# A hybrid decoder trunk on one core: the decode step's state update moved to ScalarE and an adding transfer, and Strassen pairs widened from 14 to 16 K tiles

## The chip, the cores and the metric

The kernel runs on 1 core of one Trainium2 chip. The metric is the device time of one execution in microseconds (us), lower is better. A core has a matmul engine (TensorE, PE in the profile; PEld is its weight load), VectorE (DVE), ScalarE (ACT), GpSimd (POOL) and SyncE (SP). Engines run on their own and wait for each other by semaphores; each takes its instructions in a fixed order. POOL and SP also issue DMA transfers, which 16 DMA engines carry out.

## What is computed

Two layers of a decoder trunk, for a prompt of 512 tokens and 8 samples of one new token each, all in float32:

```python
h = rmsnorm(x, norm_g)
z = h @ w_in                                # 2048 x 8192
b_c, c_c, x_c, g_c, q, k, v, g_r = split_projection(z)
conv_y, new_buf = short_conv(c_c * x_c, conv_buf, conv_w)
y_conv = b_c * conv_y * jax.nn.silu(g_c)
...
o, new_S = retention(q, k, v, ret_S, retention_log_gamma())
...
x = x + jnp.concatenate([y_conv, y_ret], axis=-1) @ w_out
x = x + jax.nn.sigmoid(x @ w_pg) * (p_i @ w_ple)
```

The part called the decode step here is the retention of the 8 samples. Each has one new position, so with L = 1 a head's state and output are

```python
S_new = jnp.exp(log_gamma) * S + jnp.einsum('blhd,blhe->bhde', k, v)    # gamma S + k v
o = S_new applied to q                                                  # one vector per head
```

with 4 heads of 256 and gamma = 1 - 2^(-5-h) for head h. There are 2 layers x 4 heads x 8 samples = 64 such steps, each on a 256 x 256 state.

## The kernel before

**Tiling.** Activations are kept turned, 128 features x 520 columns a tile (512 prompt tokens and 8 samples); 2048 features are KT = 16 such K tiles. A column block of a weight is 128 wide, and `pair` (line 396) makes the outputs of two neighbouring column blocks together. Each operand is split into a high part of float32r and a low remainder, and one product of a weight tile with half of the columns (260) is three matmuls (`mm3`, lines 247 to 249): high by high, high by low, low by high. ScalarE writes the high half of a weight chunk and VectorE the low half (`split_w`, lines 229 and 230), into a ring `split` of SPLIT = 60 tiles; raw weights are loaded by SP into a ring `raw`.

**Plain and Strassen pairs.** A pair is 2 output blocks x 2 halves of the columns. `plain` makes all four products of every K tile. `strassen` (line 290) takes the first s K tiles as two halves of s/2 and makes 7 products of s/2 tiles with sums of weights (`add`, line 319, on VectorE) and sums of operands (`operand_sums`, prepared once a layer and kept in slots) in place of 8; the remaining 16 - s tiles go by four plain products each. With s = 16 there is no remainder: it takes three PSUM banks (a, b, d) in place of four, and the result that `c` held waits in a slot. Which s a pair has is in the lists `HEADS`, `CONVS`, `OUT_ROWS` and `GATES`, one per stage, with a list for each layer. The packing of the weights on the host follows the same lists.

**Stages of a layer.** Four heads (`retain`, line 817), each with pairs for q, k, v and the gate; eight convolution blocks with two pairs each (the loop over `j`); then the output projection and the gate projection. The prompt's retention runs in nine steps (`steps`) hung between later pairs.

**The decode step.** `retain` puts a head's 8 samples on the list `todo`; `sample` (line 789) is called at the end of each head's pair, in the middle of every second one, and in the middle of the convolutions' pairs. A call finishes the sample loaded by the call before and loads the next one. `sample_load` (line 768) brings the state `sret` and the rows of k and q, spread over 128 partitions (`kq`), into two slots by POOL's queue (`SIDE`). `sample_step` (line 774) then scales the state by gamma on ScalarE (line 776), adds k times v on VectorE (line 780, two halves of 256, with v per partition as a scalar), stores the state to `o_rets` and reduces state times q on VectorE (line 784, two reductions into `osum`). After the last convolution block `sample_norm` normalises `osum`.

**Order.** The order on each engine is made when the program is built, by a scheduler with priorities; instructions passed through `keep` stay in program order among themselves. POOL's queue carries the decode step's transfers, the retention's operands (`hs`), the spilled activations (`x1s`, `x2s`, `yc`, `ys`) and some small work. `slots` is a pool of NSLOT = 75 tiles of 128 x 520.

## Time and profile before

| | |
|---|---|
| device time, median of 3 runs | 2167.58 us (2167.56 to 2169.25) |
| span of the profiled execution, first to last instruction | 2167.3 us |
| granted TensorE clock, mean | 0.999 |
| DMA traffic | 387.31 MB, mean 179 GB/s |
| heads of layer 0 and 1 | about 50 to 450 us and 1100 to 1500 us |
| convolutions of layer 0 and 1 | about 450 to 710 us and 1500 to 1750 us |

The profile is of one execution. Its page gives the span, which the prediction uses as that execution's own time; the median of the runs lies 0.3 us above it. Rows of groups read: line, engine, operation, what it writes from what it reads, shapes and count, then the busy time in us and the mean duration of one in ns, then the time that the engine stood idle just before these instructions and what ended most of it. Rows of waits read: who waited, for whom, us in total, times, the longest in us. Rows by stretch give, for each engine, busy us and instructions in brackets. Matmuls overlap in the pipeline, so PE's busy time says little on its own; the number of matmuls in a stretch does.

### The profile page before, as it was taken

The numbers are of one execution on the slowest core, as the hardware profiler recorded it, in microseconds if no ns is written. First come the engines' busy times: TensorE is split into PE (matmuls) and PEld (weight loads), VectorE is DVE, ScalarE is ACT, GpSimd is POOL, SyncE is SP. The second block draws the span as 40 slices with busy tenths as digits, with TensorE's granted clock in tenths as the row PEclk, the third lists the DMA queues.
The fourth block names the chain that finished last, engine by engine and source line by source line (L and its number), as shares of the span: only waits on it lengthen the run. The fifth ranks groups of instructions, "written<-read, shape, count | busy, mean of one in ns | idle before, by whom it ended". The sixth has DMA issues, their size and how long they took to land. (4 is left out here: it accounts for less than half of the span.)

```text
span 2167.3 us, 48178 instructions
## 1 busy us (share of the span) xinstructions
PE 2147.8 (99%) x17861; PEld 2142.1 (99%) x17861; DVE 1896.1 (87%) x3849; ACT 1264.5 (58%) x2647; POOL 430.6 (20%) x746
## 2 busy tenths in 40 slices
PE   9999999999999999999999999999999999999998
PEld 9999999999999999999999999999999999999998
DVE  8889988998999987987997988989999998879884
ACT  8656655565555655655765655565645555456565
POOL 2313222211001211200212222231111022011011
PEclk9999999999999999999999999999999999999999
DMA  8555565545543745645645566664464355566455
GB/s 288 171 175 197 181 217 184 178 157 175 158 129 118 238 156 187 215 154 160 215 144 175 172 213 191 189 209 170 151 182 149 120 158 202 176 207 200 128 164 198
DMA packets 182861, 387.31 MB, mean 179 GB/s; under 512 B 25888, under 2 KB 56352, under 8 KB 182624
## 3 DMA queue, kind: packets, MB, share of 16 engines
q1 hardware_dynamic: 128704, 212.98, 31.6%
q0 software_dynamic: 53056, 169.84, 23.8%
q8 instruction: 140, 2.29, 0.4%
q10 hardware_dynamic: 864, 1.39, 0.2%
q14 instruction: 97, 0.79, 0.1%
HBM read 318.96 MB, written 65.15 MB: 177 GB/s over the span
## 5 line engine op out<-in xcount | busy, mean ns | idle before, releaser
L247 PE MATMUL ps_g<-slot,split 128*128 128x260 f32 x5465 | 1531.6, 284 | 7.2 <-ACT slot L307 2.9
L248 PE MATMUL ps_g<-slot,split 128*128 128x260 f32 x5465 | 1534.3, 282 | 0.3 <-DVE slot L555 0.3
L249 PE MATMUL ps_g<-slot,split 128*128 128x260 f32 x5461 | 1519.9, 283 | 0.5 <-DVE split L230 0.5
L229 ACT ACTIVATE split<-raw 128x512 fp32r<-128x512 f32 (+2 forms) x1347 | 777.3, 596 | 583.1 <-DVE raw L319 213.2
L247 PEld LDWEIGHTS ps_g<-slot,split 128*128 128x128 f32 x5465 | 1024.0, 188 | 10.1 <-ACT slot L307 3.7
L248 PEld LDWEIGHTS ps_g<-slot,split 128*128 128x128 f32 x5465 | 1028.5, 188 | 0.5 <-DVE slot L555 0.5
L249 PEld LDWEIGHTS ps_g<-slot,split 128*128 128x128 f32 x5461 | 1019.8, 188 | 1.0 <-DVE split L230 1.0
L230 DVE TENSOR_TENSOR split<-raw,split 128x512 fp32r<-128x512 f32 (+2 forms) x1346 | 849.2, 652 | 172.5 <-PE ps_g L248 85.4
L319 DVE TENSOR_TENSOR raw<-raw 128x512 f32<-128x512 f32 (+1 forms) x660 | 428.9, 660 | 32.5 <-DMA raw<-wi 23.7
L307 ACT ACTIVATE slot<-ps_g 128x260 f32<-128x260 f32 x336 | 127.4, 381 | 140.6 <-PE ps_g L249 122.7
L551 ACT ACTIVATE slot<-slot 128x520 fp32r<-128x520 f32 (+1 forms) x212 | 109.2, 562 | 46.6 <-DVE slot L414 11.1
L552 DVE TENSOR_TENSOR slot<-slot,slot 128x520 fp32r<-128x520 f32 (+1 forms) x212 | 124.4, 620 | 4.1 <-ACT slot L551 3.9
L781 POOL DMA_DIRECT2D o_rets<-slot x64 | 35.3, 552 | 351.6 <-DVE slot L780 131.7
L307 DVE TENSOR_TENSOR slot<-ps_g,slot 128x260 f32<-128x260 f32 x168 | 70.9, 424 | 6.0 <-PE ps_g L249 3.7
L869 POOL DMA_DIRECT2D slot<-hs x64 | 46.2, 724 | 118.7 <-DVE split L230 42.7
L814 POOL DMA_DIRECT2D hs<-slot x64 | 35.6, 556 | 139.3 <-DVE slot L755 61.3
L780 DVE SCALAR_TENSOR_TENSOR slot<-slot,vs,slot 128x256 f32<-128x256 f32 x128 | 56.1, 481 | 4.5 <-ACT slot L776 4.3
L746 DVE TENSOR_TENSOR slot<-slot,slot 128x520 f32<-128x520 f32 x80 | 55.8, 698 | 4.7 <-DMA o_rets<-slot 3.7
L770 POOL DMA_DIRECT2D slot<-sret x64 | 35.5, 554 | 114.6 <-ACT split L229 37.3
L1058 POOL DMA_DIRECT2D slot<-x1s x76 | 40.8, 538 | 87.6 <-PE ps_g L249 27.2
L1209 POOL DMA_DIRECT2D x2s<-slot x30 | 16.4, 545 | 201.6 <-DVE slot L1204 200.6
L771 POOL DMA_DIRECT2D slot<-kq x64 | 34.9, 547 | 106.0 <-DVE slot L876 22.2
(217 smaller groups left out, 1733.8 us busy)
## 6 DMA issues: line engine op xcount, KB each, us to landing
raw<-wi SPq DMA_DIRECT2D x377, 256.0 KB, 3.9
raw<-wo SPq DMA_DIRECT2D x128, 256.0 KB, 5.4
raw<-wg SPq DMA_DIRECT2D x122, 256.0 KB, 4.1
raw<-wi SPq DMA_DIRECT2D x136, 192.0 KB, 4.0
slot<-x1s POOLq DMA_DIRECT2D x76, 260.0 KB, 5.1
slot<-sret POOLq DMA_DIRECT2D x64, 256.0 KB, 4.0
hs<-slot POOLq DMA_DIRECT2D x64, 256.0 KB, 4.0
slot<-hs POOLq DMA_DIRECT2D x64, 256.0 KB, 5.2
```

Source lines behind the costliest of these rows:

```text
L229: S.activation(hi, raw, AF.Copy)
L230: V.tensor_tensor(lo, raw, F(hi), SUB)
L247: PE.matmul(out, wh, xh, start=start, stop=False, skip_group_check=more)
L248: PE.matmul(out, wh, xl, start=False, stop=False, skip_group_check=more)
L249: PE.matmul(out, wl, xh, start=False, stop=stop, skip_group_check=more)
L307: fn(*args)
L319: V.tensor_tensor(out[:, n], x[:, n], y[:, n], op)
L551: keep(S.activation(hi, src[:, n], AF.Copy))
L552: V.tensor_tensor(lo, src[:, n], F(hi), SUB)
L746: V.tensor_tensor(out[:, n], v, table[:, n], MUL)
L780: keep(V.scalar_tensor_tensor(st[:, c], k, vs[:, h, e, b : b + 1], st[:, c], MUL, ADD))
L869: SIDE.dma_start(t[:, :512].rearrange("p (m n) -> p m n", m=2), src)
```

## The change

The decode step's sum gamma S + k v is formed in another way. ScalarE writes k times v into a fresh slot (two `Copy` activations of 256 with v as the scale), and a transfer of POOL's queue adds the state `sret` from DRAM onto it (`accum_op=ADD`). v is divided by gamma beforehand, so the slot then holds S_new / gamma; the reduction on VectorE multiplies by gamma, and ScalarE scales the slot by gamma before it is stored. A sample passes through three calls of `sample` in place of two: load k and q; add; reduce, scale and store. VectorE's two adds per sample are gone. The lists for heads and convolutions have 16 in place of 14, save the last pair of the convolutions; plain pairs and the pair with 8 stay. There is one slot more, the split ring has 56 tiles in place of 60, and the column vector `vec` is 128 wide in place of 160, since gamma is now a constant.

```diff
--- before.py
+++ after.py
@@ -27,7 +27,7 @@
 PLE = 256
 PAST = 4096
 EPS = 1e-6
-NSLOT = 75
+NSLOT = 76
 CH = 4
 CHS = 4
 CHA = 4
@@ -50,8 +50,9 @@
 EARLY = 6


-HEADS = [[0, 0, 0, 8] + [14] * 12, [0] + [14] * 15]
-CONVS = [[14] * 2 + [16] * 13 + [14]] * 2
+GAMMA = [1.0 - 2.0 ** (-5 - h) for h in range(H)]
+HEADS = [[0, 0, 0, 8] + [16] * 12, [0] + [16] * 15]
+CONVS = [[16] * 15 + [14]] * 2
 OUT_ROWS = [[0, 8, 16, 16, 16, 16, 16, 0]] * 2

 MIXED, MIX = 64, [*range(8, 14), *range(8), 14, 15]
@@ -62,7 +63,7 @@
 RAW = 32
 WARM = 8
 FIRST = 8
-SPLIT = 60
+SPLIT = 56


 def F(ap):
@@ -558,7 +559,7 @@
         return op


-    vec = const.tile([P, 160], F32, name="vec")
+    vec = const.tile([P, P], F32, name="vec")

     def norm_g(l, k):
         return vec[:, 16 * l + k : 16 * l + k + 1]
@@ -576,9 +577,6 @@
     def kd(h, m):
         c = 112 + 4 * h + m
         return vec[:, c : c + 1]
-
-    def gam(h):
-        return vec[:, 128 + h : 129 + h]

     ident = const.tile([P, P], F32, name="ident")
     ones = const.tile([P, P], F32, name="ones")
@@ -677,7 +675,7 @@
         if b == 1:
             raw = raw_ring.get(4)
             DMA.dma_start(raw.rearrange("p (m n) -> p m n", n=P), wi[0, 0:4, :, :P].rearrange("m p n -> p m n"))
-            S.dma_start(vec, vecs)
+            S.dma_start(vec, vecs[:, :P])
             x = get()
             for n in (LEFT, RIGHT):
                 DMA.dma_start(x[:, n], xT[0, :, n])
@@ -766,30 +764,36 @@
             return g

         def sample_load(h, b):
-            st, kb = get(), get()
-            SIDE.dma_start(st[:, :512], sret[l, h, b])
+            kb = get()
             SIDE.dma_start(kb[:, :512], kq[l, h, b].rearrange("c d -> (c d)").partition_broadcast(P))
-            return h, b, st, kb
-
-        def sample_step(h, b, st, kb):
-
-            keep(S.activation(st[:, :512], st[:, :512], AF.Identity, scale=gam(h)))
-            k = kb[:, 256:512]
+            return h, b, kb
+
+        def sample_add(h, b, kb):
+
+            st = get()
             for e in range(2):
                 c = slice(256 * e, 256 * e + 256)
-                keep(V.scalar_tensor_tensor(st[:, c], k, vs[:, h, e, b : b + 1], st[:, c], MUL, ADD))
-            SIDE.dma_start(o_rets[l, h, b], st[:, :512])
+                keep(S.activation(st[:, c], kb[:, 256:512], AF.Copy, scale=vs[:, h, e, b : b + 1]))
+            SIDE.dma_start(st[:, :512], sret[l, h, b], accum_op=ADD)
+            return h, b, kb, st
+
+        def sample_step(h, b, kb, st):
+
             for e in range(2):
                 c = slice(256 * e, 256 * e + 256)
-                V.tensor_tensor_reduce(k, st[:, c], kb[:, :256], 1.0, 0.0, MUL, ADD, osum[:, e, h, b : b + 1])
+                V.tensor_tensor_reduce(kb[:, 256:512], st[:, c], kb[:, :256], GAMMA[h], 0.0, MUL, ADD, osum[:, e, h, b : b + 1])
+            keep(S.activation(st[:, :512], st[:, :512], AF.Copy, scale=GAMMA[h]))
+            SIDE.dma_start(o_rets[l, h, b], st[:, :512])
             put(st, kb)

-        loaded = []
+        loaded, added = [], []

         def sample():

+            if added:
+                sample_step(*added.pop(0))
             if loaded:
-                sample_step(*loaded.pop(0))
+                added.append(sample_add(*loaded.pop(0)))
             if todo:
                 loaded.append(sample_load(*todo.pop(0)))

@@ -846,7 +850,7 @@
             vf = []
             for e, z in enumerate(head(mt + 4)):
                 t = z.slot if z.ps is None else copied(z.ps).slot
-                V.scalar_tensor_tensor(vs[:, h, e, :], t[:, SEQ:T], 1.0 / 16, rb[:, SEQ:T], MUL, MUL)
+                V.scalar_tensor_tensor(vs[:, h, e, :], t[:, SEQ:T], 1.0 / 16 / GAMMA[h], rb[:, SEQ:T], MUL, MUL)
                 vf.append(t)
             aside_copy(h, 4, vf)
             todo.extend((h, b) for b in range(NS))
@@ -1099,7 +1103,7 @@
             if j < CJ - 1:
                 middle.append(sample)
             if j == CJ - 1:
-                while loaded or todo:
+                while added or loaded or todo:
                     sample()
                 O.ready = 7
                 sample_norm(nc, small, pr, osum, onesd, half_neg, gs, lambda k: gn_g(l, k))
```

The scheduler orders the whole program anew. Of PE, 17664 rows become 17571.

The first place is SP's queue in the heads of layer 0, with the weight loads of the pairs. Line 312 (313 in the changed kernel) loads the halves of a Strassen pair's weights, line 222 (223) the K tiles left over. Before, from the pair with s = 8 through the first pair with s = 14:

```order
L312 DMA raw<-wi 128x512 x4
L222 DMA raw<-wi 128x512 x4
L312 DMA raw<-wi 128x384 x2
L312 DMA raw<-wi 128x512 x2
L312 DMA raw<-wi 128x384
L312 DMA raw<-wi 128x512
L312 DMA raw<-wi 128x384
L312 DMA raw<-wi 128x512
L222 DMA raw<-wi 128x256 x2
```

Now, from the pair with s = 8 to the last pair of the convolutions:

```order
L313 DMA raw<-wi 128x512 x4
L223 DMA raw<-wi 128x512 x4
L313 DMA raw<-wi 128x512 x216
L313 DMA raw<-wi 128x384 x2
L313 DMA raw<-wi 128x512 x2
```

The halves are 8 tiles in two loads of 4, and the loads of tiles left over are gone between the pair with 8 and the last pair.

The second place is one decode step in the convolutions of layer 0, the 28th of 64, on ScalarE and VectorE. ScalarE before, where line 776 scales the state by gamma:

```order
L229 ACTIVATE split<-raw 128x512
L776 ACTIVATE slot_417_7423<-slot_417_7423,vec 128x512
L307 ACTIVATE slot_421_7495<-ps_g 128x260
L229 ACTIVATE split<-raw 128x512 x3
L307 ACTIVATE slot_420_7494<-ps_g 128x260
```

ScalarE now, where line 785 scales the sample before this one and line 776 writes k times v of this one:

```order
L230 ACTIVATE split<-raw 128x512
L785 ACTIVATE slot_416_7261<-slot_416_7261 128x512
L776 ACTIVATE slot_421_7501<-slot_417_7265,vs 128x256 x2
L230 ACTIVATE split<-raw 128x512
L308 ACTIVATE slot_420_7335<-ps_g 128x260
L230 ACTIVATE split<-raw 128x512 x2
L308 ACTIVATE slot_419_7334<-ps_g 128x260
```

VectorE before, with the adds of line 780 and the reductions of line 784 (each of those also has a row that reads its sum out):

```order
L319 TENSOR_TENSOR raw<-raw 128x512 x2
L307 TENSOR_TENSOR slot_421_7495<-ps_g,slot_421_7495 128x260
L780 SCALAR_TENSOR_TENSOR slot_417_7423<-slot_418_7424,vs,slot_417_7423 128x256 x2
L319 TENSOR_TENSOR raw<-raw 128x512
L230 TENSOR_TENSOR split<-raw,split 128x512
L307 TENSOR_TENSOR slot_420_7494<-ps_g,slot_420_7494 128x260
L784 ISA slot_418_7424,osum<-slot_417_7423,slot_418_7424 128x256
L784 ISA osum 128x1
```

VectorE now, the same sample's reductions (slot_421_7501 is the slot that the transfer adds to):

```order
L231 TENSOR_TENSOR split<-raw,split 128x512 x3
L320 TENSOR_TENSOR raw<-raw 128x512
L231 TENSOR_TENSOR split<-raw,split 128x512 x4
L784 ISA slot_417_7265,osum<-slot_421_7501,slot_417_7265 128x256
L784 ISA osum 128x1
L784 ISA slot_417_7265,osum<-slot_421_7501,slot_417_7265 128x256
L784 ISA osum 128x1
L231 TENSOR_TENSOR split<-raw,split 128x512
L320 TENSOR_TENSOR raw<-raw 128x512 x2
```

The adds are gone. The reductions of this sample stand three weight splits behind the split that precedes its two copies on ScalarE, while the scaling by line 785 of the same sample comes a whole pair later.

The third place is POOL's queue around the same step. Before:

```order
L770 DMA slot_428_7909<-sret 128x512
L771 DMA slot_429_7910<-kq 128x512
L1112 DMA yc<-slot_414_7244 128x520
L781 DMA o_rets<-slot_417_7423 128x512
L771 DMA slot_434_8150<-kq 128x512
L770 DMA slot_433_8149<-sret 128x512
```

Now, where line 777 is the adding transfer and line 786 the store:

```order
L777 DMA slot_416_7261<-sret 128x512
L768 DMA slot_428_7751<-kq 128x512
L1116 DMA yc<-slot_413_7084 128x520
L786 DMA o_rets<-slot_416_7261 128x512
L777 DMA slot_421_7501<-sret 128x512
L768 DMA slot_433_7991<-kq 128x512
```

Before, a state's load stood samples ahead of its store and waited only for a slot; now its adding transfer stands right behind the store of the sample before, and both follow ScalarE's instructions of the same call.

## Prediction

> **What bounds the kernel now.** I read the first parts of the page, then busy time by stage, then the waits of PE.
>
> ```profile
> span 2167.3 us, 48178 instructions
> ## 1 busy us (share of the span) xinstructions
> PE 2147.8 (99%) x17861; PEld 2142.1 (99%) x17861; DVE 1896.1 (87%) x3849; ACT 1264.5 (58%) x2647; POOL 430.6 (20%) x746
> ```
>
> ```profile
> core 0: us, PE busy (x) PEld busy (x) DVE busy (x) ACT busy (x) POOL busy (x), PEclk, DMA share, GB/s
> 100.00:440.00 340.00, 340.00 (x2842) 339.93 (x2841) 306.35 (x677) 202.88 (x446) 89.32 (x154) 1.00 0.60 192
> 500.00:700.00 200.00, 200.00 (x1672) 200.00 (x1671) 181.12 (x359) 106.14 (x213) 23.30 (x32) 1.00 0.48 144
> 1180.00:1500.00 320.00, 319.33 (x2670) 318.83 (x2669) 285.91 (x640) 187.07 (x415) 84.51 (x143) 1.00 0.60 190
> ```
>
> ```profile
> PE ps_g L247 <- ACT slot L307: 2.9, 4, 1.3
> PE ps_g L247 <- ACT ps_g L307: 1.6, 2, 1.2
> PE ps_g L247 <- ACT split L229: 1.5, 2, 1.3
> ```
>
> The three stretches are the heads of layer 0, its convolutions, and the heads of layer 1. A matmul's busy time overlaps its neighbour's, so 99% alone proves little; the count does. The first stretch starts one matmul every 340.00 / 2842 = 119.6 ns and the second one every 200.00 / 1672 = 119.6 ns, at a granted clock of 1.00: the same pitch in two stages whose other work differs. PE's largest wait is 2.9 us in the whole run. So TensorE sets the end nearly everywhere, and time goes only with matmuls or comes back as new PE waits. VectorE is second, at 306.35 / 340.00 = 90.1% in the heads and 181.12 / 200.00 = 90.6% in the convolutions.
>
> **The matmuls.** A pair by `strassen` with s = 14 makes 7 products of 7 tiles and 4 products of the 2 tiles left over, (49 + 8) x 3 = 171 matmuls; with s = 16 it makes 7 x 8 x 3 = 168. The lists change 12 + 15 pairs of the heads and 2 + 2 of the convolutions: 31 pairs, 93 matmuls, 93 x 119.6 ns = **11.1 us** off PE. No cover is needed for this: PE is the bound, and in the convolutions 13 of 16 pairs already run at s = 16 with that same pitch.
>
> **VectorE, ScalarE and the queues.**
>
> ```profile
> L230 DVE TENSOR_TENSOR split<-raw,split 128x512 fp32r<-128x512 f32 x1031 | 695.0, 690 | 147.8 <-PE ps_g L248 81.2 <-ACT split L229 51.8 <-issue 6.1
> L319 DVE TENSOR_TENSOR raw<-raw 128x512 f32<-128x512 f32 x520 | 354.1, 688 | 17.6 <-DMA raw<-wi 12.1 <-DMA raw<-wo 2.9
> L230 DVE TENSOR_TENSOR split<-raw,split 128x384 fp32r<-128x384 f32 x249 | 137.1, 555 | 16.2 <-ACT split L229 9.9 <-PE ps_g L248 3.4 <-ACT slot L551 1.9
> L319 DVE TENSOR_TENSOR raw<-raw 128x384 f32<-128x384 f32 x140 | 77.4, 554 | 14.9 <-DMA raw<-wi 11.6 <-DMA raw<-wg 2.8
> L230 DVE TENSOR_TENSOR split<-raw,split 128x256 fp32r<-128x256 f32 x66 | 27.3, 423 | 8.5 <-ACT split L229 7.6 <-PE ps_g L248 0.8
> L307 ACT ACTIVATE slot<-ps_g 128x260 f32<-128x260 f32 x336 | 127.4, 381 | 140.6 <-PE ps_g L249 122.7 <-DVE osum L784 4.6 <-DVE slot L746 4.3
> L780 DVE SCALAR_TENSOR_TENSOR slot<-slot,vs,slot 128x256 f32<-128x256 f32 x128 | 56.1, 481 | 4.5 <-ACT slot L776 4.3
> L776 ACT ACTIVATE slot<-slot,vec 128x512 f32<-128x512 f32 x64 | 45.7, 714 | 0.0
> L1263 ACT ACTIVATE slot<-slot,vec 128x256 f32<-128x256 f32 x16 | 7.5, 498 | 2.5 <-DMA slot<-x2s 1.6 <-DVE slot L1275 1.0
> ```
>
> VectorE, per changed pair: the 4 weight sums grow from 0.554 + 0.688 to 2 x 0.688, together +0.54 us; the splits go from 7 x (0.555 + 0.690) + 2 x 0.423 = 9.56 to 14 x 0.690 = 9.66, +0.10. That is +0.64 us, 31 times, +19.8 us. The decode step loses both adds of each of 64 samples, 56.1 us; its reductions stay. Net -36 us, so in mean load VectorE is relieved.
>
> ScalarE: one eviction less per pair (0.381), splits alike (within 0.1), so about -14 us. The 128 new copies, 128x256 with a scale from a column, are not in this trace; the nearest row, L1263, has the same size and kind of scale at 0.498: +64 us. The scaling of the state stays, about 0.1 us cheaper with a constant. Net about +44 on 1264.5 us, some 60% of the span, and its idle time hides it.
>
> SP issues 8 loads of 128x512 per changed pair instead of 10 smaller ones, with the same bytes. POOL issues as many transfers as before; if the adding one costs twice a load's 0.54 us, 64 x 0.54 = 35 us come onto an engine that is 20% busy. The split ring goes from 60 tiles to 56: at 8 tiles (hi and lo) a chunk that is 7 chunks instead of 7 and a half, so at most half a chunk, 6 matmuls = 0.7 us, of PE's stock; at nothing, since 7 chunks of 12 matmuls still are 10 us.
>
> One more operand sum (8 instead of 7) has to stand before the first big pair of the heads in each layer. It exists later anyway, so the work is only earlier: at most its VectorE time of about 3 us (four 260-wide operations at 0.43, two splits at 0.70), twice. Nothing to 6 us; I take **1 us**, since PE holds a stock of split weights of several us there.
>
> **The new wait.** This is the step that can undo the rest. Before, the state was loaded a whole call of `sample` ahead, and the step found it there. Now the reduction on VectorE waits for the adding transfer, which POOL can issue only after ScalarE's two copies. The order of the changed kernel puts that reduction, in all 64 places, 0 to 5 weight splits (median 2) behind the copies, not a call later; what stands behind it on VectorE are weight splits and sums for PE. How long is the way, and when does VectorE arrive?
>
> ```profile
> L770 POOL DMA_DIRECT2D slot<-sret x64: 537/544/585, 50.5 to 1670.9; - x64
> DMA to landing us min/median/max: 2.8/4.0/7.3
> ```
>
> ```profile
> o_rets<-slot POOLq DMA_DIRECT2D x64, 256.0 KB, 3.1
> ```
>
> ```profile
> 599.37 0.61 ACT L229 ACTIVATE split<-raw 128x512 fp32r<-128x512 f32 x1
> 599.88 0.71 ACT L776 ACTIVATE slot<-slot,vec 128x512 f32<-128x512 f32 x1
> 600.50 1.14 ACT L229 ACTIVATE split<-raw 128x512 fp32r<-128x512 f32 x2
> ...
> 602.67 1.14 ACT L229 ACTIVATE split<-raw 128x512 fp32r<-128x512 f32 x2
> ```
>
> ```profile
> L776 ACT ACTIVATE slot<-slot,vec x64: 706/713/722, 81.2 to 1713.3; 128x512 f32<-128x512 f32 x64
> ```
>
> ```profile
> 602.38 1.29 DVE L230 TENSOR_TENSOR split<-raw,split 128x512 fp32r<-128x512 f32 x2
> 603.59 0.70 DVE L1108 TENSOR_TENSOR slot<-slot,slot 128x520 f32<-128x520 f32 x1
> 604.20 1.29 DVE L230 TENSOR_TENSOR split<-raw,split 128x512 fp32r<-128x512 f32 x2
> ```
>
> The way: the trace has no adding transfer. Its bounds are a plain load of the same tile, 4.0 us from issue to landing, and a load and a store one after the other, 4.0 + 3.1 = 7.1 us. I take **5.0 us**, nearer to the load, because it is one transfer with one landing. The arrival: at 599.88 ScalarE does the sample's instruction just behind the split that ends at 599.98. VectorE does the low half of that same split only at 602.38; three splits further, where the changed order has the reduction at this sample, it is through at 605.49. Had the copies ended at 599.88 + 2 x 0.5 = 600.9, VectorE would have arrived 4.6 us later. The same reckoning at the 64 ScalarE steps of L776, the first at 81.2 and the last at 1713.3 us, each with its own distance from the changed order, gives a median of 3.5 us, with a tenth below 1.4 and a tenth above 5.4. So VectorE would stand still for about 5.0 - 3.5 = 1.5 us at a sample.
>
> What that costs, by the groups of the first stretch, 100 to 440 us, and ScalarE's waits in it:
>
> ```profile
> L247 PE MATMUL ps_g<-slot,split 128*128 128x260 f32 x845 | 239.3, 284 | 0.0
> ```
>
> ```profile
> ACT split L229 <- PE ps_g L248: 22.1, 33, 2.3
> ACT split L229 <- PE ps_g L249: 20.2, 34, 1.8
> ```
>
> A third of a pair's 171 matmuls stand in line 247, 57, so the stretch holds 845 / 57 = 14.8 pairs of 340 / 14.8 = 22.9 us, the retention included. VectorE is idle for 9.9% of that, 2.3 us a pair. `sample` is called at the end of each pair and in the middle of every second one; with these 1.5 samples a pair the removed adds give 1.5 x 2 x 0.481 = 1.4 us, the sums and splits take 0.64, the shorter pair 0.36: 2.7 us a pair, or **1.8 us a sample**, is what VectorE can lose without falling behind PE. In the convolutions it is one sample a pair, with 9.4% of 20 us + 0.96 = 2.8 us. A stall of 1.5 us stays under both. ScalarE waits 33 + 34 times for PE to free a split buffer in that stretch, so the ring is often full, and PE's stock of some six chunks, 6 x 12 x 0.1196 = 8.6 us, rides over a single long one. So I cost it at nothing; the cover is VectorE's idle tenth, and it is thin.
>
> The Trainium skill, "Collectives: The Full Stack", section "The bandwidth ceiling: the fold count and why AG ≠ RS ≠ AR", speaks against the adding transfer: an add by the DMA engines needs two source reads through the same ring, so it halves the rate. With "DMA: Bandwidth & Descriptors", section "Anatomy of one DMA — SWDGE (gpsimd) path", where a transfer is about 2.0 us + bytes / 436e3 per us, doubling 256 KB adds an estimated 0.6 us, 4.6 instead of 4.0 us here; the stall would then be 1.1 us and the sum the same. No run shows an adding transfer yet, and the plain load's 4.0 us is longer than the 2.6 us that this formula makes of it.
>
> **The sum.** 2167.3 - 11.1 + 1.0 = 2157.2 us of span. The median of the runs shown, 2167.58, is 0.3 us above the profiled span, so **2157.5 us**.
>
> **The rivals.**
> 1. *VectorE becomes the bound* (slower). If the adding transfer takes the upper bound, 7.1 us, a sample stalls VectorE by 3.6 us, 1.8 more than the heads can bear: 1.8 x 1.5 = 2.7 us for each of about 12 head pairs with samples, 32 us a layer, less the stock of 8.6 us that refills between layers: 2 x 24 = 48 us, and 2205 us in all. It decides from a landing of 3.5 + 1.8 = 5.3 us on; at 6.3 us it costs 2 x (1.0 x 1.5 x 12 - 8.6) = 19 us, 2176. For it: the bounds straddle the point, and plain loads already reach 7.3 us. Against it: a late VectorE arrives later at the next reduction as well, so the stall partly limits itself.
> 2. *Part of the gain is given back* in single PE waits: long landings that meet an empty stock, retention operands fetched late because POOL queues them behind the adding transfer and the store that now waits for ScalarE. 4 to 11 us back, 2161 to 2168 us.
> 3. *More than the count.* Three banks instead of four at a pair's end and fewer evictions could remove the 6.0 us of PE waits quoted above: down to 2151 us.
> That the lists take effect is not in doubt: the PE order is 93 rows shorter.
>
> **How the numbers follow.** Forecast (2154 to 2161) 0.60; rival 2 0.16; rival 1 0.19; rival 3 0.05. A measurement of this kernel tells 0.2%, 4.3 us, from no change: below 2163.2 is faster, above 2171.9 slower. Faster is the forecast, rival 3 and a third of rival 2: 0.70. Same is the rest of rival 2 and the mildest of rival 1: 0.13. Slower 0.17. The range runs from 2152 to 2176: it holds the forecast, rival 2 and the mild end of rival 1, and leaves out about 0.15 above and 0.02 below.
>
> **What would show it.** Right: PE keeps 119.6 ns a matmul in the heads, with 93 fewer; VectorE shows new waits for the transfer from `sret` at L784, 1 to 2 us each and below 120 us in all; ScalarE about 1308 us busy. The landing row of that transfer decides: near 5 us or below, and the forecast stands; above 5.3, VectorE's idle tenth in the heads should be gone and PE should wait for the low halves of `split`. Wrong in the sums: a PE wait of 1 to 3 us around 95 us and around 1140 us of the span.

## The result and the profile after

| | before | changed |
|---|---|---|
| device time, median | 2168.41 us | 2241.32 us (2240.14 to 2245.27, 4 runs) |
| ratio, 95% interval | | 1.0339 (1.0325 to 1.0354) |
| span of the profiled execution | 2167.3 us | 2239.3 us (2241.17 us of device time) |

The changed kernel is 3.4% slower. The forecast was 2157.5 us with a range up to 2176: it had the sign wrong. In the changed kernel most lines of the helpers have moved by one: the products of `mm3` are L248 to L250, the splits L230 (ScalarE) and L231 (VectorE), the evictions of PSUM L308, the weight sums L320. The decode step's copies are L776, its adding transfer L777, its reductions L784, the scaling L785 and the store L786.

The head of the page after, and busy time in the same three stretches as before (heads of layer 0, its convolutions, heads of layer 1):

```profile
span 2239.3 us, 47851 instructions
...
PE 2168.1 (97%) x17768; PEld 2152.4 (96%) x17768; DVE 1869.2 (83%) x3659; ACT 1295.4 (58%) x2682; POOL 456.3 (20%) x746
```

```profile
100.00:440.00 340.00, 321.96 (x2611) 318.41 (x2610) 281.66 (x574) 199.56 (x423) 95.56 (x150) 0.98 0.61 180
500.00:700.00 200.00, 192.38 (x1588) 190.72 (x1586) 168.74 (x324) 110.60 (x234) 25.82 (x39) 1.00 0.48 147
1180.00:1500.00 320.00, 307.91 (x2516) 305.30 (x2516) 264.19 (x530) 185.10 (x386) 85.69 (x134) 0.98 0.60 180
```

PE has its 93 matmuls fewer, 17768 for 17861, but it starts 2611 in the first stretch where it started 2842: one every 340 / 2611 = 130.2 ns in place of 119.6. VectorE is *less* busy, 82.8% of the first stretch where it was 90.1%. So no engine has become full; PE stands still at times, and for what is in the view of waits (who waited for whom, us in all, times, the longest):

```profile
PE ps_g L248 <- DVE slot L308: 21.4, 17, 4.3
PE ps_g L250 <- DVE split L231: 17.1, 13, 2.8
PE ps_g L248 <- ACT split L230: 9.3, 4, 2.9
...
DVE split L231 <- ACT split L230: 169.7, 198, 4.8
DVE slot L784 <- DMA slot<-sret: 95.8, 43, 4.4
```

Of before, the same view had 2.9 us as PE's longest row. Now PE waits most for VectorE: for evictions of its PSUM banks and for low halves of weights. VectorE's own new wait is the one for the adding transfer, 95.8 us in all. The transfer's issues, and the time from issue to landing:

```profile
L777 POOL DMA_DIRECT2D slot<-sret x64: 847/884/982, 101.7 to 1785.7; - x64
DMA to landing us min/median/max: 3.8/6.4/9.7
```

It lands after 6.4 us in the median, where the plain load of before took 4.0. One place shows the whole chain, the change of heads at 1511 to 1530 us. These are rows of the timeline after (start, duration, engine and line, then in brackets how long the engine had stood idle and for whom), from the sample's copies on; ScalarE, GpSimd, VectorE and PE apart:

```profile
1509.63 0.90 ACT L776 ACTIVATE slot<-slot,vs 128x256 f32<-128x256 f32 x2
...
1511.34 0.90 POOL L777 DMA_DIRECT2D slot<-sret  x1
...
1516.41 0.69 DVE L231 TENSOR_TENSOR split<-raw,split 128x512 fp32r<-128x512 f32 x1 [0.90 <-ACT split L230]
1521.03 0.43 DVE L784 CUSTOM_DVE_ANT_0 slot<-slot,slot 128x256 f32<-128x256 f32 x1 [3.92 <-DMA slot<-sret]
1521.38 0.08 DVE L784 DVE_READ_ACCUMULATOR2_ANT osum<- 128x1 f32 x1
1521.38 0.69 DVE L320 TENSOR_TENSOR raw<-raw 128x512 f32<-128x512 f32 x1
1521.98 0.42 DVE L784 CUSTOM_DVE_ANT_0 slot<-slot,slot 128x256 f32<-128x256 f32 x1
1522.33 0.08 DVE L784 DVE_READ_ACCUMULATOR2_ANT osum<- 128x1 f32 x1
1522.33 0.69 DVE L231 TENSOR_TENSOR split<-raw,split 128x512 fp32r<-128x512 f32 x1
1522.93 0.68 DVE L320 TENSOR_TENSOR raw<-raw 128x512 f32<-128x512 f32 x1
1523.53 0.42 DVE L308 TENSOR_TENSOR slot<-ps_g,slot 128x260 f32<-128x260 f32 x1
...
1524.01 0.59 PE L248 MATMUL ps_g<-slot,split 128*128 128x260 f32 x1 [4.26 <-DVE slot L308]
```

The transfer is issued at 1511.34 and its reader starts at 1521.03, 9.7 us later. For the last 3.92 us of that VectorE stands: the reduction is next in its order, and nothing behind it may go first. Behind it in the queue stands the eviction L308, whose PSUM bank PE needs for its next product. When the transfer is there, the reductions and three weight instructions still go first, and PE, which has waited 4.26 us by then, gets the bank. The same stretch as busy time, before, during and after the wait:

```profile
1517.00:1521.00 4.00, 2.75 (x24) 2.54 (x22) 0.11 (x1) 0.75 (x3) 0.00 (x0) 1.00 1.02 308
1521.00:1523.40 2.40, 0.00 (x0) 0.00 (x0) 2.37 (x7) 0.96 (x3) 0.04 (x1) 0.97 0.74 286
1523.40:1530.00 6.60, 5.99 (x27) 6.00 (x28) 6.19 (x14) 3.33 (x8) 1.39 (x2) 0.50 0.46 96
```

Two things more are to be seen. The DMA engines are full in the four us of the wait (a share of 1.02, 308 GB/s). And when PE may go on, its granted clock is 0.50 for 6.6 us: 27 matmuls where 6.6 / 0.1196 = 55 would fit.

**The sum over the run.** I added up, over all neighbouring matmuls whose starts lie more than 0.26 us apart, what exceeds the pitch of 0.1196 us: 75.9 us after, 15.4 before. The trace's clock records show half clock for 49.1 us after (11 pieces, all but the last of 3.41 or 6.83 us) and for 5.1 before (at the end). In 6.0 us of the pieces after PE stood anyway, so that half clock slowed its work for 44.0 - 6.0 = 38.0 us more than before, and cost half of that. So 2167.3 - 11.1 (matmuls) + 60.5 (standing still) + 38.0 / 2 (clock) = 2235.7 us, against a span of 2239.3; 3.6 us stay open. Within that the matmul saving is there, and some 80 us came against it. The share of the clock is this execution's: it had a mean clock of 0.989, another one with 0.993 had a span of 2238.3 us.

### The profile page after: what moved, and what is told of

It reads as the page before. It is cut to its first block, busy times and chain, and to the rows that moved or that the text cites. A ratio compares the mean times of both kernels' runs of the same rounds, so it can differ in the third digit from the quotient of the medians.

```text
span 2239.3 us, 47851 instructions
## 1 busy us (share of the span) xinstructions
PE 2168.1 (97%) x17768; PEld 2152.4 (96%) x17768; DVE 1869.2 (83%) x3659; ACT 1295.4 (58%) x2682; POOL 456.3 (20%) x746
## 5 line engine op out<-in xcount | busy, mean ns | idle before, releaser
L248 PE MATMUL ps_g<-slot,split 128*128 128x260 f32 x5434 | 1536.1, 286 | 36.6 <-DVE slot L308 21.4
L250 PE MATMUL ps_g<-slot,split 128*128 128x260 f32 x5430 | 1529.0, 284 | 17.2 <-DVE split L231 17.1
L230 ACT ACTIVATE split<-raw 128x512 fp32r<-128x512 f32 (+1 forms) x1285 | 782.1, 624 | 733.9 <-PE ps_g L249 317.4
L248 PEld LDWEIGHTS ps_g<-slot,split 128*128 128x128 f32 x5434 | 1025.7, 190 | 45.5 <-DVE slot L308 25.2
L250 PEld LDWEIGHTS ps_g<-slot,split 128*128 128x128 f32 x5430 | 1025.7, 190 | 20.6 <-DVE split L231 20.4
L231 DVE TENSOR_TENSOR split<-raw,split 128x512 fp32r<-128x512 f32 (+1 forms) x1284 | 850.6, 679 | 177.1 <-ACT split L230 169.7
L320 DVE TENSOR_TENSOR raw<-raw 128x512 f32<-128x512 f32 (+1 forms) x660 | 439.9, 680 | 12.3 <-DMA raw<-wi 9.4
L308 ACT ACTIVATE slot<-ps_g 128x260 f32<-128x260 f32 x336 | 124.6, 371 | 37.2 <-PE ps_g L250 19.5
L784 DVE CUSTOM_DVE_ANT_0 slot<-slot,slot 128x256 f32<-128x256 f32 x128 | 53.7, 420 | 100.3 <-DMA slot<-sret 95.8
L786 POOL DMA_DIRECT2D o_rets<-slot x64 | 35.5, 555 | 368.3 <-ACT slot L785 269.1
L308 DVE TENSOR_TENSOR slot<-ps_g,slot 128x260 f32<-128x260 f32 x168 | 70.7, 421 | 6.8 <-PE ps_g L250 4.8
L777 POOL DMA_DIRECT2D slot<-sret x64 | 57.1, 892 | 45.3 <-ACT slot L776 25.6
L776 ACT ACTIVATE slot<-slot,vs 128x256 f32<-128x256 f32 x128 | 57.7, 498 | 2.0 <-DMA ys<-slot 1.0
```

Source lines behind the costliest of these rows:

```text
L230: S.activation(hi, raw, AF.Copy)
L231: V.tensor_tensor(lo, raw, F(hi), SUB)
L248: PE.matmul(out, wh, xh, start=start, stop=False, skip_group_check=more)
L250: PE.matmul(out, wl, xh, start=False, stop=stop, skip_group_check=more)
L308: fn(*args)
L320: V.tensor_tensor(out[:, n], x[:, n], y[:, n], op)
```

## The experiments

The main theory is the one just read off: VectorE's queue stands at the reduction and holds up evictions and low halves. Its rivals: the lists of 16 cost VectorE more than they save PE; the ring of 56 tiles, taken as free, is not; and the order of the changed program is worse as such, whatever waits in it. Of the kernel before, the medians beside these 16 runs were 2167.1 to 2169.8 us. "Early" below is the reduction where the change has it, "late" one call of `sample` later.

### The parts of the change alone

`e1_lists` is the kernel before with the new lists only, `e2_decode` the changed kernel with the old lists:

```diff
-HEADS = [[0, 0, 0, 8] + [14] * 12, [0] + [14] * 15]
-CONVS = [[14] * 2 + [16] * 13 + [14]] * 2
+HEADS = [[0, 0, 0, 8] + [16] * 12, [0] + [16] * 15]
+CONVS = [[16] * 15 + [14]] * 2
```

> The lists of 16 alone, on the kernel before (decode step, slots and split ring as before). Theory A (the reduction that waits for the adding transfer blocks VectorE, and behind it PSUM evacuations and low halves for PE): 2157 us, between 2153 and 2162, 11 us of matmuls off and no new PE waits. Rival B (pairs of 16 in the heads cost it themselves, since a bank is now freed by VectorE in the middle of a pair): above 2200 us. Rival C (the adding transfer's queue and traffic delay other loads): 2157 us as A.

> The changed decode step alone, with the lists of before (and the changed kernel's slots and ring of 56). Theory A: most of the loss stays, 2190 to 2240 us, VectorE waits 60 to 120 us for the transfer from sret, and the clock drops after long PE waits. Rival B: about 2168 us. Rival C: 2190 us or more.

`e1_lists` took 2186.19 us, ratio 1.0071 (1.0054 to 1.0087): not the 11 us of the count faster, but 16 slower. `e2_decode` took 2238.22 us, 1.0315 (1.0300 to 1.0331): the decode step, with ring and slots, makes nearly the whole loss without the lists. For `e1_lists` no theory had this time: the main one said 2157. In the first stretch of `e1_lists`:

```profile
100.00:440.00 340.00, 331.15 (x2752) 329.24 (x2751) 312.34 (x646) 196.15 (x400) 92.27 (x156) 1.00 0.57 188
```

VectorE stands at 312.34 / 340 = 91.9% there and PE loses 90 matmuls; in the convolutions, where the lists change 2 pairs of 16, it loses one (1671 for 1672). To see whether that is VectorE's load, `e5_lists_light` takes load off it: `e1_lists` without the two adds of each decode step (the state's outer product is left out):

```diff
-                keep(V.scalar_tensor_tensor(st[:, c], k, vs[:, h, e, b : b + 1], st[:, c], MUL, ADD))
```

> The lists of 16 alone, as in e1_lists, and the two adds of k times v on VectorE left out of every decode step (the state is then only gamma times the old one): 56 us less on VectorE, all transfers and waits as before the change. Theory D (e1_lists lost 27 us against the count because VectorE, at 92% of the heads, has no idle time left to catch up after a burst): 2155 to 2168 us, PE waits as before. Rival B (three banks and VectorE's eviction in the middle of a pair cost it, whatever VectorE's load): 2180 us or more.

It took 2163.36 us, 0.998 (0.997 to 0.999), 23 us less than `e1_lists`:

```profile
100.00:440.00 340.00, 337.54 (x2813) 336.32 (x2812) 304.26 (x618) 201.64 (x410) 90.88 (x157) 1.00 0.60 194
```

With VectorE back at 304.26 / 340 = 89.5% PE starts 2813 matmuls there. That speaks for VectorE's load as what the lists of 16 cost under the old decode step; without it they bring 4 us of the 11. It is not shown, since the program's order changed too: 6080 of PE's 17768 rows stand elsewhere in the two traces, and one slot more, which loads no engine, costs 16 us below.

### The reduction a call later, and a shorter transfer

`e3_late` leaves the changed kernel as it is, but has ScalarE scale and store first and VectorE reduce the scaled state, so that the order puts the reduction behind the scaling of the following call:

```diff
-            for e in range(2):
-                c = slice(256 * e, 256 * e + 256)
-                V.tensor_tensor_reduce(kb[:, 256:512], st[:, c], kb[:, :256], GAMMA[h], 0.0, MUL, ADD, osum[:, e, h, b : b + 1])
             keep(S.activation(st[:, :512], st[:, :512], AF.Copy, scale=GAMMA[h]))
             SIDE.dma_start(o_rets[l, h, b], st[:, :512])
+            for e in range(2):
+                c = slice(256 * e, 256 * e + 256)
+                V.tensor_tensor_reduce(kb[:, 256:512], st[:, c], kb[:, :256], 1.0, 0.0, MUL, ADD, osum[:, e, h, b : b + 1])
```

`e4_plain` keeps the place but loads the state in place of adding it (the outer product is left out of the result):

```diff
-            SIDE.dma_start(st[:, :512], sret[l, h, b], accum_op=ADD)
+            SIDE.dma_start(st[:, :512], sret[l, h, b])
```

> The changed kernel with the two reductions placed behind ScalarE's scaling of the state, so a call of sample later; same instructions, same transfers. Theory A: 2155 to 2172 us, VectorE's waits for sret at the reduction gone (below 15 us for ScalarE's scaling in their place), PE waits below 25 us in all, clock share 0.995 or more. Rivals B and C: 2225 us or more, since neither the pairs nor the transfers change.

> The changed kernel with a plain load from sret in place of the adding transfer: the outer product of k and v is left out of the state, all places and waits are as in the changed kernel. It measures the transfer: landing 4.0 us as before in place of 6.4. Theory A: VectorE's waits for it fall to a third of 96 us or less, 2170 to 2200 us. Rival B: 2240 us. Rival C by the traffic of the add: 2160 to 2180 us.

`e3_late` took 2177.88 us, 1.0036 (1.0023 to 1.0049): 63 us of the loss gone by moving the reduction, though not the 2155 to 2172 us that were expected. The transfer still lands after 6.2 us in the median; the waits for it are now these:

```profile
ACT slot L782 <- DMA slot<-sret: 26.2, 16, 3.1
...
DVE slot L786 <- ACT slot L782: 18.2, 12, 3.5
```

ScalarE, with some 40% to spare, bears most of the wait. `e4_plain` took 2197.50 us, 1.0132 (1.0115 to 1.0149). In the same place a plain load lands after 5.2 us (4.0 was expected), and VectorE waits half as long for it (a third was expected); here are also PE's waits for VectorE:

```profile
DVE slot L784 <- DMA slot<-sret: 49.1, 31, 3.8
```

```profile
PE ps_g L250 <- DVE split L231: 7.3, 9, 1.4
PE ps_g L248 <- DVE slot L308: 4.0, 6, 2.0
```

This run settles the main cause, because it is the only one that leaves the order alone: row by row, its trace has the same instructions in the same order as the changed kernel's, on PE (17768), VectorE (3662), ScalarE (2691) and GpSimd (753). What changed is the transfer, with its issue (0.54 us on GpSimd, 0.88 before the edit). VectorE waits 95.8 - 49.1 = 46.7 us less for it, PE's waits for evictions fall from 21.4 to 4.0 us and those for low halves from 17.1 to 7.3, and the kernel takes 43.8 us less. Faster transfers of other data are not behind it: the weight loads `raw<-wi` land after 4.6 us in the median where they took 4.8, and PE's wait for ScalarE's halves stays (9.1 us, 9.3 before the edit). With a landing near the 5.0 us that the prediction assumed, 28 us of loss against the kernel before remain; this run does not divide them between the 49.1 us that VectorE still waits, the ring, the slot and the lists.

`e6_late_old_lists` is `e3_late` with the lists of before:

> The late reduction of e3_late with the lists of before. Theory D: the relief of VectorE alone is worth little where PE already kept its pitch: 2165 to 2172 us; the lists of 16 on top (e3_late, 2178) then cost 6 to 13 us although they take 11 us of matmuls away. If instead the late reduction itself still stalls: 2178 to 2190 us, and the lists bring their 11 us.

It took 2175.22 us, 1.0036 (1.0023 to 1.0049), between its two expectations: with the late reduction, lists of 14 or 16 differ by 3 us only, and neither meets the kernel before.

### The wait for the transfer taken out

A later reduction changes the order too. `e13_no_wait` keeps the reductions in the changed kernel's call of `sample` and takes from them only the tile of the adding transfer; `e17_no_wait_60` does the same with the ring of 60 tiles:

```diff
-                V.tensor_tensor_reduce(kb[:, 256:512], st[:, c], kb[:, :256], GAMMA[h], 0.0, MUL, ADD, osum[:, e, h, b : b + 1])
+                V.tensor_tensor_reduce(kb[:, 256:512], kb[:, :256], kb[:, :256], GAMMA[h], 0.0, MUL, ADD, osum[:, e, h, b : b + 1])
```

> The changed kernel with its reductions, in the same place, reading the k and q rows in place of the sum, so that VectorE no longer waits there for the adding transfer (the reduction of the state is left out, the reductions' number and size stay). If VectorE's wait with its queue behind it is the cause of the 63 us that the later reduction saved: 2170 to 2190 us, no wait of VectorE for sret, and the waits of TensorE for VectorE's evictions (21 us) below 5 us. If it is the order of instructions around the early reduction and not the wait: 2225 to 2245 us.

> The same with the split ring of 60 tiles, against 2209 us of the changed kernel with that ring. If the wait is the cause there too, it saves less, as less is lost: 2165 to 2187 us, no better than the late reduction with that ring (2185 us). If the losses by wait and by ring simply add, 2209 - 63 = 2146 us.

`e13_no_wait` took 2177.19 us, 1.0049 (1.0034 to 1.0063): 64 us less than the changed kernel. PE's waits in it, the largest first, and VectorE's at the reduction:

```profile
PE ps_g L248 <- ACT split L230: 7.6, 7, 2.6
...
PE ps_g L250 <- DVE split L231: 2.0, 3, 1.4
...
PE ps_g L248 <- DVE slot L308: 0.9, 2, 0.7
```

```profile
DVE slot L784 <- ACT slot L776: 23.1, 12, 3.7
```

The waits for VectorE's evictions fell from 21.4 to 0.9 us and those for its low halves from 17.1 to 2.0. The place was not kept, however. Without the wait for the transfer the scheduler makes another order (2718 of PE's 17768 rows and 1243 of VectorE's 3662 stand elsewhere), and VectorE comes to the reduction 0.7 us after the copies' end in the median, where in the changed kernel it came 4.7 us after it; it then waits for the copies, 23.1 us. So this run agrees with `e4_plain`, and by itself doesn't tell the wait from the order. `e17_no_wait_60` took 2166.10 us, 0.9998 (0.9988 to 1.0007), which is 43 us below the same kernel with the wait (2208.88, next section). It lies in the range of the first expectation, but it is better than the late reduction with that ring (2185), which was not expected; and the losses do not simply add (2146).

The price of a microsecond that VectorE stood at the reduction can be read only where the order is the same, from the changed kernel to `e4_plain`: 43.8 / 46.7 = 0.94 us at the end.

### The ring, the slots, and what is left

The change's two sizes alone, on the kernel before: `e7_ring` has both, `e10_ring_only` and `e12_slot_only` one each.

```diff
-NSLOT = 75
+NSLOT = 76
-SPLIT = 60
+SPLIT = 56
```

> The kernel before with one slot more and a split ring of 56 tiles; decode step and lists as before. Theory E (the ring and the slot, which every kernel with the changed decode step shares, cost the PE waits and clock drops at the change from convolutions to output projection): 2174 to 2180 us, with a PE wait near 3 us at about 725 and 1800 us. Otherwise the ring is free: 2165 to 2170 us.

> The kernel before with the split ring of 56 tiles, the slots left at 75: the one half of the ring and slot experiment (2201 us). If the ring of an even number of chunks costs the time (it ends with ScalarE waiting for TensorE's last read of a chunk and VectorE waiting for ScalarE): 2195 to 2205 us, with VectorE's waits for ScalarE's split near 155 us. If the slot is the cause by another order of the same work: within 5 us of 2168 us.

> The kernel before with 76 slots in place of 75, nothing else: the other half. If the ring is the cause of the 33 us: 2165 to 2172 us. If any other order that the scheduler makes costs this kernel some tens of us, since the order of before is an unusually good one: 2180 us or more.

`e7_ring` took 2201.26 us, 1.0150 (1.0134 to 1.0167); the ring alone 2188.52, 1.0098 (1.0080 to 1.0115); the slot alone 2184.32, 1.0078 (1.0059 to 1.0098). `e7_ring` lies above both of its expectations. My expectations for the halves took ring and slot for each other's rivals, but both cost, 20 and 16 us: the ring alone fell between its two, the slot alone met its second (2180 us or more). The ring leaves a mark that can be read. Waits of VectorE in the low split, before and with the ring alone:

```profile
DVE split L230 <- PE ps_g L248: 85.4, 109, 2.2
...
DVE split L230 <- ACT split L229: 69.3, 77, 4.7
```

```profile
DVE split L230 <- ACT split L229: 169.6, 206, 4.6
...
DVE split L230 <- PE ps_g L248: 18.0, 28, 2.0
```

With 56 tiles, 14 groups of 4, VectorE waits for ScalarE's high half where it waited for PE to free a buffer; with 60, 15 groups, both halves share that wait; all runs with 56 have 143 to 182 us in this row, all with 60 have 37 to 72. The changed kernel's 169.7 us in this row are the ring's mark, then, and not the decode step's: `e13_no_wait` has 175.1 us there at 2177 us. It is the largest wait that VectorE has after the change, and the wrong one to follow.

The same two ring sizes under the other variants, and the lists of 14 or 16 under each:

```diff
-SPLIT = 56
+SPLIT = 60
```

`e8_late_60` is `e3_late` with it, `e9_after_60` the changed kernel, `e11_late_60_old_lists` is `e6_late_old_lists`, `e15_decode_60` is `e2_decode`. `e16_late_77` is `e3_late` with `NSLOT = 77`.

> The late reduction of e3_late with the split ring back at 60 tiles (76 slots, lists of 16). Theory E: 2160 to 2170 us, the long PE waits near 725 and 1790 us gone. Otherwise 2175 to 2181 us, as e3_late.

> The changed kernel with the split ring of 60 tiles in place of 56. If the ring's loss, which the ring and slot experiment measured as 33 us, adds to the loss by the reduction placed early: about 2208 us. If the early reduction alone holds VectorE up and the ring only decides which engine's waits show it: 2230 to 2245 us, and the waits of VectorE for ScalarE's high half fall from 170 us to below 100 while its waits for TensorE rise. The transfer from sret still lands in 6.0 to 6.8 us (median) either way.

> The changed decode step with its reduction a call later, the lists of 14 of before, and the ring of 60 (slots 76): the run with the ring of 56 was at 2175 us. If the ring costs something of its own in any arrangement: 2155 to 2168 us, and this beats or meets the kernel before (2168 us). If its effect depends on the order around it, as the run with the lists of 16 and the ring of 60 suggests (2185 against 2178 us with 56): 2170 to 2185 us. VectorE about 1840 us busy in both.

> The changed decode step with the early reduction, the lists of 14 of before and the ring of 60: against 2209 us with lists of 16. If the 93 matmuls that the lists save reach the end once the ring is right: 2218 to 2222 us. If they are given back by VectorE's larger sums: 2200 to 2212 us.

> The changed kernel with the later reduction and one slot more (77, ring 56), against 2178 us with 76. If slots that come free late hold the order up: 2160 to 2172 us. If a slot more is only another order, as in the kernel before, where it cost 16 us: 2172 to 2195 us.

Measured, in us, with the ratio to the kernel before and its interval in brackets; all have 76 slots unless it is said:

| reduction | lists | ring 56 | ring 60 |
|---|---|---|---|
| early | 16 | 2241.32, the change | 2208.88 (1.0173 to 1.0207) |
| early | 14 | 2238.22 | 2241.74 (1.0332 to 1.0362) |
| late | 16 | 2177.88; 77 slots: 2188.03 (1.0083 to 1.0113) | 2185.27 (1.0043 to 1.0096) |
| late | 14 | 2175.22 | 2174.91 (1.0020 to 1.0045) |
| early, no wait | 16 | 2177.19 | 2166.10 |
| of before | 14 | 2201.26; 75 slots: 2188.52 | 2184.32; 75 slots: the kernel before |
| of before | 16 | | 75 slots: 2186.19 |

Read by columns, the ring of 60 is worth 32 us in the first row, costs 4 and 7 in the next two, does nothing in the fourth, and is worth 11 and 17 (20 with 75 slots) below. Read by pairs of rows, 16 for 14 is worth 33 us in one pair and costs 3 to 16 in the others. No size has a price of its own. `e9_after_60` met its expectation of 2208 us, but `e15_decode_60` missed both of its own by 20 us and more, and `e8_late_60` and `e16_late_77` repaired nothing. What does hold throughout the table is the first reading: each kernel whose early reduction waits for the adding transfer lies at 2209 to 2242 us, and each one without that wait at 2166 to 2201. No version that does the whole computation beat the kernel before; the nearest is `e11_late_60_old_lists`, 0.3% behind it.

What stays open is why the orders without the wait differ among themselves by up to 35 us. Each size makes another order of the whole program, and the traces show the loss as a few short stops at changing places (`e12_slot_only`, say, has 25.4 us of the gaps defined above against 15.4 before). I did not find one mechanism for them.

## Why the prediction was wrong

**The matmuls: right.** 17768 is 93 fewer, and the sum over the run comes out nearer with their 11.1 us (3.6 us short) than without them (7.5 us over). But no run shows them reaching the end whole: where the lists alone differ, the time moves by what else the new order brings.

**VectorE, ScalarE and POOL as loads: right.** VectorE 1869.2 us busy, forecast 1896.1 - 36 = 1860; ScalarE 1295.4, forecast 1308; the copies took 498 ns each, as their neighbour did. POOL's adding issue took 0.88 us against 0.54, less than double.

**The sums, 1 us: no loss there.** PE has no gap of 0.6 us or more around 95 and 1140 us. (The 0.3 us from span to median set one execution's span against other executions; an execution's device time is 1.7 to 2.2 us above its own span in these runs. It changes nothing here.)

**The stall's size: right by luck; its price: wrong.** VectorE waits 95.8 us for the transfer, 95.8 / 64 = 1.5 us a sample, the forecast stall, but two errors cancel in it: the landing was 6.4 us and not 5.0, and VectorE came 4.7 us after the copies and not 3.5 (medians; the transfer was issued 0.3 us after them, which the forecast left out). It was also not spread evenly: 43 samples waited, 2.2 us each. So a sign named for the forecast being right, waits "below 120 us in all", held while the forecast failed. The step that failed is the next one: "So I cost it at nothing; the cover is VectorE's idle tenth, and it is thin." 46.7 of the 95.8 us cost 43.8 us, with the order unchanged (`e4_plain`); the kernels without the whole of the wait are 63 and 64 us faster, by an order that differs too. Three things were wrong in the step.

First, it compared means: 1.5 us of stall a sample against 1.8 us of idle time. VectorE's idle time was no store of free time; most of it stood where VectorE waited for PE or ScalarE in the low split (85.4 and 69.3 us in the kernel before), and a wait for a transfer elsewhere need not fall into it. After the change VectorE is idle for 17% of the heads of layer 0, and PE waits for it all the same.

Second, "PE's stock of some six chunks ... rides over a single long one" counted only split weights as what stands behind the reduction. Behind it stand evictions as well: L308 at 1523.53, above. For the PSUM bank there is no stock here; PE needs it at the pair's next product. That is PE's largest new wait, 21.4 us.

Third, a stop of PE has a price beyond its length, about 19 us over the run by the half clock. The profile before could not show it, since PE never stopped for long. The Trainium skill, "TensorE: Matmul & The Clock Gate", section "HAM oscillation — how this bites in real kernels", has the rule that gaps above about 3.4 us bring the clock down; here gaps of 2.10 to 3.09 us did (next but one section), so the rule would have kept this price at nothing for most of them.

**The ring, "at most half a chunk, 0.7 us ... at nothing": wrong.** On the kernel before the ring alone cost 20 us, and with the slot, which the prediction did not price, 33. The reckoning looked at how much stock the ring holds; it left out that another size makes another order, and that another engine then waits for it. In the changed kernel the ring makes 32 us (2241.32 to 2208.88), and 11 in the kernels without the wait for the transfer. Why is not shown: with 60 tiles VectorE waits longer for the transfer (109.7 us), and the kernel is faster all the same.

**The rivals.** Rival 1 had the sign and the place. Its threshold (a landing of 5.3 us) was crossed, but its mechanism, VectorE as the bound, isn't what happened: VectorE is at 83%, and its idle tenth in the heads grew where it "should be gone". PE did wait for low halves, as it said. Its price at 6.3 us was 19 us, 2176 in all; the kernel at 6.4 us lies 65 us above that. It subtracted the slack and the stock, which gave little cover, and left out evictions and clock. Rival 2 named single long landings, but priced them at 4 to 11 us.

**The adding transfer's time.** The bounds, 4.0 and 7.1 us, held the 6.4 us; I took 5.0 as nearer to the load, and the middle of the two ends, 5.6, would have been nearer. The estimate worked out from the Trainium skill ("DMA: Bandwidth & Descriptors", section "Anatomy of one DMA — SWDGE (gpsimd) path", with the add counted as double the bytes), 4.6 us, was lower still; no run shows that doubling. Not all of it is the adding: in the same place a plain load takes 5.2 us, against 4.0 a call ahead. The traffic of that moment may be why; no run shows it. So the landing was mis-sized too, and it mattered: 5.2 in place of 6.4 us is worth 43.8 us. The range would have failed without that error as well, since `e4_plain` with 5.2 us lies at 2197.50.

## What to carry to other kernels

Before a wait goes into an in-order queue, list what is queued behind it and who needs that first: an eviction of PSUM had no stock here, and the mean idle time of the waiting engine is no cover for it. If the data come from a transfer, let an engine with time to spare meet it first (here ScalarE's scaling, a whole call later, was worth 63 us, a new order included), or put the reader a fixed piece of work later. And in a kernel whose order fits this closely, every size that changes the order is a change to be measured by itself: one slot more cost 16 us.

## What the hardware showed that was not expected

The granted clock fell to half after short stops. After gaps in PE's starts of 2.10 us (at 369.2), 2.93 us (420.7) and 2.10 us (1648.6) it was 0.5 for 3.41 us, and after two close together, 3.09 and 3.00 us (166.1 and 170.3), for 6.83; after one of 2.95 us (463.2) it stayed at 1.00. So a stop of 2 to 3 us may cost 1.7 us more, but need not. The pieces are one or two times 3.41 us; the Trainium skill, "TensorE: Matmul & The Clock Gate", section "What's actually happening", describes windows of 3413 ns that run freely of the kernel, and these lengths agree with it.

The traces show more of it. In the changed kernel's trace all changes of the clock stand whole multiples of 3.413 us apart. I cut all 18 traces, from 20 us on, into such windows and added up for each window at full clock how long PE stood in it (gaps as defined above). All 39 windows with 2.0 us or more were followed by half clock; of those with 0.5 to 2.0 us, 404 were not and 10 were, nine of these with 1.88 us or more and one with 1.58. The stop of 2.95 us at 463.2 lay across a boundary, at 461.73, with 1.3 and 1.5 us on its sides.

A 256 KB transfer that adds a DRAM tile onto one in SBUF landed after 3.8 to 9.7 us, 6.4 in the median, where the plain load took 5.2 in the same place and 4.0 a call ahead; its issue on GpSimd took 0.88 us against 0.54.
